# One priority block fewer for every pair but the first, and an earlier fetch of the last four tiles of x

## The chip, the cores and the metric

The kernel runs on one core of a Trainium2 chip. The metric is the device time of one execution in microseconds, median of several runs. PE is TensorE (matrix products), DVE VectorE, ACT ScalarE, POOL GpSimd and SP SyncE, which here only issues DMAs. Each engine works through its own queue in a fixed order and waits there for semaphores.

## What is computed

One layer of an encoder on 1024 tokens of 1024 features, all in float32: a feed-forward at half weight, a mixing layer (bidirectional retention and neighbourhood attention behind one combined projection), and a second feed-forward at half weight, each between two RMS norms. The change concerns the feed-forwards:

```python
def _rms_norm(x, gain):
    xf = x.astype(jnp.float32)
    y = xf * lax.rsqrt(jnp.mean(xf * xf, axis=-1, keepdims=True) + RMS_EPS)
    return (y * gain.astype(jnp.float32)).astype(x.dtype)

def _swiglu(x, w_in, w_out):
    g, u = jnp.split(x @ w_in, 2, axis=-1)
    return (jax.nn.silu(g) * u) @ w_out
...
        h = _swiglu(_rms_norm(x, ffn1_pre_norm[l]), ffn1_w_in[l], ffn1_w_out[l])
        x = x + 0.5 * _rms_norm(h, ffn1_post_norm[l])
...
        h = _swiglu(_rms_norm(x, ffn2_pre_norm[l]), ffn2_w_in[l], ffn2_w_out[l])
        x = x + 0.5 * _rms_norm(h, ffn2_post_norm[l])
```

`w_in` is 1024 x 5632 and `w_out` 2816 x 1024.

## The kernel before

**Products.** A float32 number is split into a high part h, rounded to the format in which PE is fast, and the rest l: a cast on ACT (L61) and a subtraction on DVE (L62), or on POOL where the code says so. A product of two split operands is three matmuls, h·h, h·l and l·h (`mm3`, L86 to L90). Large products use Winograd's form of Strassen's scheme: the operands are cut into quarters, and seven products of combined quarters replace eight. The combined left operands are called a11, a12, a22, s1, s2, s3 and s4.

**The input half of a feed-forward** (`ffn_in`, L517) runs over 22 pairs. Pair i is a block of 128 gate columns and the 128 up columns that belong to it. `Pairs.run` (L476) fetches the pair's two weight blocks g and u (`raw`, three buffers `wraw`, 512 KB each), forms the four combinations t1 (L490), t2 (L491), t3 (L499) and t4 (L508) on DVE, splits each right operand when its product needs it (`piece`, seven buffers `wh` and seven `wl`), and makes the products in the order a11, s2, a12, s3, s1, a22, s4. Each has 12 matmuls of 512 columns into one of six PSUM banks. After each, DVE adds the bank into the result (L494, L497, L502, L505 and L506, L510, L513). `done` applies SiLU to a gate half (ACT, L530) and multiplies it by the up half (DVE, L532) into the tile `gt`, which has three buffers. L473 holds t1 and t3 of a pair on DVE behind the s3 sum (L502) of the pair before.

For some pairs the products a11 and a12 are made ahead by `lead` (L436), before all left operands exist: pairs 0 to 2 are held in PSUM, further ones are saved (7 pairs in all in the first feed-forward, 4 in the second). Those pairs have five products left.

**The factors.** The gated result is the left operand of the output half. Two pairs (a couple) give one block of rows, for which `LeftFactors` makes the seven operands a11 to s4: four sums or differences (DVE, L557) and seven splits (ACT, L577, four buffers `gth`; DVE, L578), each of which POOL's queue stores to DRAM in two DMAs (L68; tensors g0a, g0s in the first feed-forward, g1a, g1s in the second). They are traced one by one between the products of the following pair (`between`, `step`), and what is left when the following pair is finished is traced at once (`drain`).

**The output half** (`ffn_out`) loads quarters of `w_out` (tiles x in the first feed-forward, w in the second), splits them (`wh<-x`, `wl<-x`), loads the stored factors (`g`) and multiplies. Its first three operands are built in a block with offset 80, and the last couple's sums and factors are put behind them on their engines.

**What sets the order.** The queue of each engine is fixed when the program is built. Every instruction gets a number in the order in which the code traces it. The planner goes through a modelled time line; an engine that is free takes, of the instructions that are ready by the model, the one with the lowest number. `high_priority(offset=n)` sets the counter back by n at its start, and at its end restores the value that it had at the start. With offset 0 the instructions inside keep their numbers, but what follows the block starts again from the number of the block's beginning. In `ffn_in` every pair stands in such a block (L533): offset 40 for pair 0, offset 0 for all others. The numbers of neighbouring pairs therefore overlap almost wholly, since only what is traced outside the block moves the counter on. The mixing layer uses the same `Pairs.run` without a block (L1332).

**The beginning** (`first_factors`, L298). SP fetches the first four tiles of x by rows, then in turn four pieces of the transposed x (X^T) for the first 512 tokens (`load(0, k)`, tiles b) and, by `amid`, three weight blocks of W, those of pairs 3, 4 and 5 (`fetch`). For the first two of them `fetch` also makes the first split, on POOL. The norm of the first half comes from sums of squares on ACT and DVE; the scaled X^T is split into a11 and a12. Then the last four tiles of x are fetched as eight halves (tiles `cmb` and `lead`, L355) and squared on ACT (L356), and the second half of X^T is fetched (L359). `rstd(1)` (L360, with L326 on DVE) needs all eight sums. After that s3, s2, s1, a22 and s4 are made.

Of the kernel before, what the change touches and what calls it, by code (L numbers as in the profile page):

```python
# [1 line left out]

# [1 line left out]

# [14 lines left out]
P = 128  # L19
# [217 lines left out]
class Winograd:  # L237
# [25 lines left out]
    def put(self, t, g, pt):  # L263
        c, nc = self.c, self.c.nc
        ts = slice((t % 4) * P, (t % 4 + 1) * P)
        if t < 4:
            c.split(*self.part(("a11", "a12")[g], ts), pt)
            return

        def tmp():  # L270
            return self.tmp.tile([P, 4, P], F32, tag="cmb", name="cmb", bufs=4)

        h1, l1 = [q.bitcast(F32) for q in self.part("a11", ts)]
        h2, l2 = [q.bitcast(F32) for q in self.part("a12", ts)]

        if g == 0:
            self.a21, self.s3 = tmp(), tmp()
            nc.scalar.copy(self.a21, pt)
            if self.spill is not None:
                c.store(self.spill[:, :, ts], self.a21)  # L280
            eng = nc.gpsimd if t in self.s3_on_pool else nc.vector
            eng.tensor_tensor(self.s3, h1, self.a21, ALU.subtract)
            eng.tensor_tensor(self.s3, self.s3, l1, ALU.add)
            return
        a21, s3 = self.a21, self.s3
        s1 = a21 if self.spill is None else tmp()
        c.split(*self.part("a22", ts), pt)
        nc.vector.tensor_tensor(s1, pt, a21, ALU.add)
        c.split(*self.part("s3", ts), s3)
        nc.vector.tensor_tensor(s3, pt, s3, ALU.subtract)  # L290
        c.split(*self.part("s1", ts), s1)
        c.split(*self.part("s2", ts), s3)
        nc.gpsimd.tensor_tensor(s3, h2, s3, ALU.subtract)
        nc.gpsimd.tensor_tensor(s3, s3, l2, ALU.add)
        return lambda: c.split(*self.part("s4", ts), s3, eng=nc.gpsimd)


def first_factors(c, wx, pool, halves, small, x, xt, gain, amid):  # L298

    nc = c.nc
    tt, stt = nc.vector.tensor_tensor, nc.vector.scalar_tensor_tensor
    col, ss = small[:, :KT], small[:, KT:KT + 4 * 4].rearrange("p (q t) -> p q t", q=4)
    blocks = {n: pool.tile([P, 4, 512], F32, name=n) for n in ("b11", "b21", "b22", "b12")}
    rows = [blocks[n].rearrange("p (t k) f -> p t (k f)", t=2)[:, t] for n in ("b21", "b22") for t in range(2)]

    def quarter(h, k):
        return blocks[("b11", "b12", "b21", "b22")[2 * h + k // 4]]

    def block(h, k):
        return quarter(h, k)[:, k % 4]

    def part(n, k):
        return [q[:, k] for q in wx.op(n)]

    def load(h, k):

        nc.sync.dma_start(quarter(h, k)[:, k % 4:k % 4 + 2], xt[h, k // 2])

    def rstd(h):

        rb = c.bank("pt", 2)
        with c.tc.high_priority(offset=100):
            if h:
                tt(ss[:, 1], ss[:, 1], ss[:, 2], ALU.add)  # L326
            nc.vector.tensor_scalar(ss[:, h], ss[:, h], EPS, None, ALU.add)
            r = c.rstd(ss[:, h], 4)
            for t in range(4):
                nc.tensor.transpose(rb[:, t * P:(t + 1) * P], r[:, t:t + 1].to_broadcast([P, P]), c.ident)  # L330
        return rb

    def scale(h, k, rb):
        stt(block(h, k), block(h, k), col[:, k:k + 1], rb, op0=ALU.mult, op1=ALU.mult)

    for t in range(4):
        nc.sync.dma_start(rows[t], x[t * P:(t + 1) * P, :])
    nc.sync.dma_start(col, gain)
    for t in range(4):
        out = ss[:, 0, t:t + 1]  # L340
        if t % 2:
            nc.vector.tensor_tensor_reduce(rows[t], rows[t], rows[t], scale=1.0 / D, scalar=0.0, op0=ALU.mult,
                                           op1=ALU.add, accum_out=out)
        else:
            nc.scalar.activation(rows[t], rows[t], AF.Square, scale=1.0 / 32.0, accum_out=out)
    rb = rstd(0)
    for k in range(0, KT, 2):
        load(0, k)
        amid(k // 2)
    for k in range(KT):  # L350
        scale(0, k, rb)
        c.split(*part(("a11", "a12")[k // 4], k % 4), block(0, k))
    for t in range(4):
        for b in range(2):
            nc.sync.dma_start(halves[t][b], x[(t + 4) * P:(t + 5) * P, b * 512:(b + 1) * 512])  # L355
            nc.scalar.activation(halves[t][b], halves[t][b], AF.Square, scale=1.0 / 32.0,  # L356
                                 accum_out=ss[:, 1 + b, t:t + 1])
    for k in (0, 4, 2, 6):
        load(1, k)  # L359
    rb = rstd(1)  # L360
    yield


    for k in range(4):
        a11, a12, a21, a22 = block(0, k), block(0, k + 4), block(1, k), block(1, k + 4)
        scale(1, k, rb)
        scale(1, k + 4, rb)
        tt(a11, a11, a21, ALU.subtract)
        c.split(*part("s3", k), a11)
        tt(a11, a22, a11, ALU.subtract)  # L370
        c.split(*part("s2", k), a11)
        yield
    for k in range(4):
        a21, a22 = block(1, k), block(1, k + 4)
        tt(a21, a21, a22, ALU.add)
        c.split(*part("s1", k), a21)
    for k in range(4):
        a11, a12, a22 = block(0, k), block(0, k + 4), block(1, k + 4)
        c.split(*part("a22", k), a22)
        nc.gpsimd.tensor_tensor(a12, a12, a11, ALU.subtract)  # L380
        c.split(*part("s4", k), a12, eng=nc.gpsimd)
# [132 lines left out]
        done(2)  # L514


def ffn_in(c, pairs, pool, put):  # L517


    nc = c.nc  # L520
    pairs.between = put.step
    pairs.end, last = None, []
    for i in range(FT):
        gate = [pool.tile([P, 512], F32, tag=f"c{j}", name=f"c{j}", bufs=2) for j in range(2)]
        gt = pool.tile([P, S], F32, tag="gt", name="gt", bufs=3)
        up = gt[:, :512], gt[:, 512:]

        def done(j):
            if j < 2:
                nc.scalar.activation(gate[j], gate[j], AF.Silu)  # L530
            if j in (1, 2):
                last[:] = [pairs.end, nc.vector.tensor_tensor(up[j % 2], gate[j % 2], up[j % 2], ALU.mult).ins]  # L532
        with c.tc.high_priority(offset=0 if i else 40):  # L533
            pairs.run(i, (*gate, *up).__getitem__, done)
        put(i, gt)
    put.drain()
    return last + put.traced
# [634 lines left out]
def trunk_layer(ctx: ExitStack, tc, x, xt, g1a, w1i, w1o, g1b, gma, wmt, wnv, wrv, logits, dtab, rope, bias,  # L1172
                wro, wno, wmo, gmb, g2a, w2i, w2o, g2b, out):
    nc = tc.nc
# [5 lines left out]
    c = Core(tc, const, wpool, psum, dram)  # L1180
# [6 lines left out]
    gl = [{n: dram.tile([FT // 2, P, 1024], F32, name=f"g{i}{n}") for n in Winograd.NAMES} for i in range(2)]  # L1187
# [14 lines left out]
    def pool(stack, name, side="left"):  # L1202
        return stack.enter_context(tc.tile_pool(name=name, bufs=1, side=side, reuse_waits="tile"))
# [3 lines left out]
    early = pool(right, "early", "right")  # L1207
    wx = Winograd(c, apool, early, None, order=("s4", "a22", "s3", "a12", "s1", "s2", "a11"))
    with tc.tile_pool(name="norm1", bufs=1, reuse_waits="tile") as ep:
        def lead():  # L1210
            return early.tile([P, 512], F32, tag="lead", name="lead", bufs=6)

        halves = [[early.tile([P, 4, P], F32, tag="cmb", name="cmb", bufs=4).rearrange("p k t -> p (k t)")
                   for _ in range(2)] for _ in range(2)] + [[lead() for _ in range(2)] for _ in range(2)]
        fin = Pairs(c, wx, [(w1i[i], w1i[FT + i]) for i in LeftFactors.order], 3, 3)
        steps = first_factors(c, wx, ep, halves, pad, x, xt, g1a,
                              lambda j: j < 3 and fin.fetch(3 + j, nc.gpsimd if j < 2 else None))
        next(steps)
        fin.lead(lead, [lambda: next(steps)] * 4, (3, 4, 0), 2, 1)
        for _ in steps:  # L1220
            pass
    g0 = pool(left, "gl10")
    with tc.tile_pool(name="fin1", bufs=1, reuse_waits="tile") as fp:
        tail = ffn_in(c, fin, fp, LeftFactors(c, early, fp, gl[0]))
    right.close()

    spool = pool(left, "s1")
# [10 lines left out]
    ahead = {}  # L1238
# [217 lines left out]
    with tc.tile_pool(name="ep2", bufs=1, reuse_waits="tile") as ep:  # L1456
        rest = c.out_proj(KT, stream(c, gs, lambda k: d["m"][k]), lambda k: c.load_w(wmo[k]),
                          Ep(c, ep, gmb, g2a, False, rows(x1), rows(x2), wx.put))
        fin = Pairs(c, wx, [(w2i[i], w2i[FT + i]) for i in LeftFactors.order], 3, 1)
# [9 lines left out]
    with tc.tile_pool(name="fin2", bufs=1, reuse_waits="tile") as fp:  # L1469
        tail = ffn_in(c, fin, fp, LeftFactors(c, cmb, fp, gl[1]))  # L1470
# [90 lines left out]
```

## Time and profile before

| | |
|---|---|
| median of 3 runs | 2355.51 us (2354.34 to 2355.54) |
| the profiled execution's own time | 2359.59 us |
| its span, first to last instruction | 2357.8 us |
| mean granted PE clock | 0.980 |
| DMA over the span | 444.11 MB, 188 GB/s |

The first feed-forward's input half runs from about 60 to 480 us, its output half to about 700; the mixing layer follows until about 1700; the second feed-forward's input half runs from there to about 2130.

The page gives the busy time of each engine; a profile of one execution is a list of instructions with start and length, and what ended the idle time before each, inferred from semaphores. "[6.06 <-ACT wh L61]" behind a row says that the engine was idle for 6.06 us and that a cast by ACT into `wh`, line 61, ended that. Matmuls overlap, so a full PE shows them 0.222 us apart though each is listed with about 0.39 us. A few matmul records can be missing. A table of stretches gives for each engine the busy time and, behind the x, the number of instructions.

### The profile page before, as it was taken

How to read it: one execution, taken by the hardware profiler on the slowest of the kernel's cores; microseconds unless marked ns; L12 is line 12 of the kernel's file. 1: busy time of each engine (PE TensorE's matmuls, PEld its weight loads, DVE VectorE, ACT ScalarE, POOL GpSimd, SP SyncE). 2: the span in 40 equal slices, each digit the busy share in tenths (PEclk: the TensorE clock that was granted, in tenths of full speed). 3: DMA queues.
4: the chain of work that ended last, by engine and by line, in shares of the span. 5: the costliest groups of instructions: out<-in, count | busy, mean ns of one | idle time of the engine just before them, and what ended most of it. 6: DMA issues, size and time to landing. Idle time of an engine off the chain costs nothing.

```text
span 2357.8 us, 30279 instructions
## 1 busy us (share of the span) xinstructions
PE 2237.6 (95%) x10232; PEld 1838.0 (78%) x10232; DVE 1683.4 (71%) x2918; ACT 1007.2 (43%) x2086; POOL 660.2 (28%) x789
## 2 busy tenths in 40 slices
PE   6989999989998999999999999999898999998997
PEld 4767888868886887777888888887577887887886
DVE  7787977754458668869876677448977897775444
ACT  5333433332335223248876675226533343333232
POOL 3021221158624134411001222002501122115942
PEclk9999999989999999999999999999898999999999
DMA  6253443598645442267654576856434354349864
GB/s 224 97 176 125 173 170 121 190 367 295 205 161 187 170 165 99 102 195 229 217 186 145 164 217 227 312 184 213 129 108 155 130 188 160 131 171 346 303 231 167
DMA packets 149514, 444.11 MB, mean 188 GB/s; under 512 B 18736, under 2 KB 46512, under 8 KB 147248
## 3 DMA queue, kind: packets, MB, share of 16 engines
q1 hardware_dynamic: 110640, 314.23, 39.7%
q0 software_dynamic: 38720, 127.96, 14.3%
q8 instruction: 81, 1.33, 0.2%
q14 instruction: 73, 0.60, 0.1%
HBM read 305.80 MB, written 140.51 MB: 189 GB/s over the span
## 4 chain that ended last, share of the span: by engine, by line
PE 51%; issue 23%; DVE 9%; POOL 6%; DMA 3%; ACT 2%; POOLq 0%; SPq 0%; DVEq 0%; ACTq 0%
PE ps L88 15%; PE ps L90 15%; PE ps L89 15%; DVE wl L62 2%; POOL g1s L68 1%; PE pt L90 1%; PE pt L88 1%; PE pt L89 1%; POOL g1a L68 1%; POOL g0s L68 1%; POOL g0a L68 1%; PE ps L887 1%; PE pt L906 1%; DMA wraw<-in_dram 1%; DMA g<-g0a 1%
## 5 line engine op out<-in xcount | busy, mean ns | idle before, releaser
L62 DVE TENSOR_TENSOR wl<-wraw,wh 128x512 fp32r<-128x512 f32 x510 | 366.9, 742 | 131.7 <-ACT wh L61 129.8
L61 ACT CAST wh<-wraw 128x512 fp32r<-128x512 f32 x516 | 302.8, 618 | 339.9 <-PE ps L89 135.2
L88 PE MATMUL ps<-wh,g 128*128 128x512 f32 x484 | 190.5, 395 | 13.8 <-ACT wh L61 13.8
L89 PE MATMUL ps<-wl,g 128*128 128x512 f32 x484 | 190.7, 394 | 4.6 <-DVE wl L62 4.6
L90 PE MATMUL ps<-wh,g 128*128 128x512 f32 x484 | 190.0, 393 | 0.0
L62 DVE TENSOR_TENSOR wl<-x,wh 128x512 fp32r<-128x512 f32 x77 | 73.8, 974 | 93.2 <-ACT wh L61 93.0
L62 DVE TENSOR_TENSOR wl<-w,wh 128x512 fp32r<-128x512 f32 x77 | 70.5, 929 | 97.5 <-ACT wh L61 97.4
L88 PE MATMUL ps<-a11h,wh 128*128 128x512 f32 x276 | 112.0, 406 | 7.2 <-ACT wh L61 7.2
L88 PEld LDWEIGHTS ps<-wh,g 128*128 128x128 f32 x484 | 92.0, 190 | 33.9 <-ACT wh L61 14.9
L88 PE MATMUL ps<-s2h,wh 128*128 128x512 f32 x232 | 94.5, 407 | 18.9 <-ACT wh L61 15.1
L89 PEld LDWEIGHTS ps<-wl,g 128*128 128x128 f32 x484 | 91.9, 190 | 25.1 <-DVE wl L62 6.1
L90 PE MATMUL ps<-a11h,wl 128*128 128x512 f32 x276 | 110.5, 401 | 0.9 <-POOL wl L62 0.8
L89 PE MATMUL ps<-a11l,wh 128*128 128x512 f32 x276 | 109.9, 399 | 0.0
L90 PE MATMUL ps<-a12h,wl 128*128 128x512 f32 x276 | 108.1, 392 | 1.9 <-DVE wl L62 1.9
L88 PE MATMUL ps<-a22h,wh 128*128 128x512 f32 x280 | 109.7, 392 | 0.0
L88 PE MATMUL ps<-a12h,wh 128*128 128x512 f32 x276 | 108.9, 395 | 0.6 <-DVE gt L506 0.6
L89 PE MATMUL ps<-a22l,wh 128*128 128x512 f32 x280 | 109.1, 390 | 0.0
L90 PE MATMUL ps<-a22h,wl 128*128 128x512 f32 x280 | 109.0, 389 | 0.0
L89 PE MATMUL ps<-a12l,wh 128*128 128x512 f32 x276 | 107.9, 391 | 0.2 <-DVE a12l L62 0.2
L90 PEld LDWEIGHTS ps<-wh,g 128*128 128x128 f32 x484 | 92.0, 190 | 19.1
L61 ACT CAST wh<-t 128x512 fp32r<-128x512 f32 x58 | 36.0, 621 | 149.1 <-DVE t L491 147.9
L61 ACT CAST wh<-w 128x512 fp32r<-128x512 f32 x77 | 46.8, 620 | 117.6 <-PE pt L90 52.8
(424 smaller groups left out, 6497.4 us busy)
## 6 DMA issues: line engine op xcount, KB each, us to landing
wraw<-in_dram SPq DMA_DIRECT2D x218, 512.0 KB, 4.1
g<-g0s SPq DMA_DIRECT2D x44, 512.0 KB, 4.4
g<-g1s SPq DMA_DIRECT2D x44, 512.0 KB, 4.5
g<-g0a SPq DMA_DIRECT2D x33, 512.0 KB, 3.4
g<-g1a SPq DMA_DIRECT2D x33, 512.0 KB, 4.5
g0s<-gth POOLq DMA_DIRECT2D x44, 256.0 KB, 3.0
g0s<-cmb POOLq DMA_DIRECT2D x44, 256.0 KB, 2.8
g1s<-gth POOLq DMA_DIRECT2D x44, 256.0 KB, 3.1
```

The lines of the kernel that those rows point to most:

```text
L61: self.done = [nc.scalar.copy(h, src).ins, (eng or nc.vector).tensor_tensor(l, src, hf, ALU.subtract).ins]
L62: (eng or nc.vector).tensor_tensor(l, src, hf, ALU.subtract).ins]
L68: self.nc.gpsimd.dma_start(dst, src)
L88: mm(ps, a[0], b[0], start=start, stop=False)
L89: mm(ps, a[0], b[1], start=False, stop=False)
L90: mm(ps, a[1], b[0], start=False, stop=stop)
L887: nc.tensor.matmul(bv, q[:, rg * P:(rg + 1) * P], k, start=n == 0, stop=n == 1)
L906: nc.tensor.transpose(pt[:, j * P:(j + 1) * P], s[:, i % 2, (i // 2) * P:(i // 2 + 1) * P], c.ident)
```

## The change

Two things. `ffn_in` gets a parameter `ahead`, by default 0: only pair 0, and only where `ahead` is given, is built in a priority block; all others are traced without one. The first feed-forward passes 40, the second nothing. In `first_factors` the fetches of the last four tiles of x come before the third block of W, and before the scaling of the first half; the second half of X^T is fetched directly behind that block of W. The squares stay where they were.

```diff
-from contextlib import ExitStack
+from contextlib import ExitStack, nullcontext
...
     for k in range(0, KT, 2):
         load(0, k)
-        amid(k // 2)
+        if k < 4:
+            amid(k // 2)
+    for t in range(4):
+        for b in range(2):
+            nc.sync.dma_start(halves[t][b], x[(t + 4) * P:(t + 5) * P, b * 512:(b + 1) * 512])
+    amid(2)
+    for k in (0, 4, 2, 6):
+        load(1, k)
     for k in range(KT):
         scale(0, k, rb)
         c.split(*part(("a11", "a12")[k // 4], k % 4), block(0, k))
     for t in range(4):
         for b in range(2):
-            nc.sync.dma_start(halves[t][b], x[(t + 4) * P:(t + 5) * P, b * 512:(b + 1) * 512])
             nc.scalar.activation(halves[t][b], halves[t][b], AF.Square, scale=1.0 / 32.0,
                                  accum_out=ss[:, 1 + b, t:t + 1])
-    for k in (0, 4, 2, 6):
-        load(1, k)
     rb = rstd(1)
...
-def ffn_in(c, pairs, pool, put):
+def ffn_in(c, pairs, pool, put, ahead=0):
...
-        with c.tc.high_priority(offset=0 if i else 40):
+        with c.tc.high_priority(offset=ahead) if ahead and i == 0 else nullcontext():
             pairs.run(i, (*gate, *up).__getitem__, done)
...
-                              lambda j: j < 3 and fin.fetch(3 + j, nc.gpsimd if j < 2 else None))
+                              lambda j: fin.fetch(3 + j, nc.gpsimd if j < 2 else None))
...
-        tail = ffn_in(c, fin, fp, LeftFactors(c, early, fp, gl[0]))
+        tail = ffn_in(c, fin, fp, LeftFactors(c, early, fp, gl[0]), 40)
```

The second feed-forward's call stays as it is, so its pair 0 loses the block with offset 40.

## The prediction

> **What bounds the kernel now.** I read the page's busy shares first, then the table of stretches, which is where this change can be priced.
>
> ```profile
> span 2357.8 us, 30279 instructions
> PE 2237.6 (95%) x10232; PEld 1838.0 (78%) x10232; DVE 1683.4 (71%) x2918; ACT 1007.2 (43%) x2086; POOL 660.2 (28%) x789
> ```
>
> TensorE is the bound over the whole span: nothing that shortens another engine pays unless it fills a hole on PE. So the next view is PE by stretches. The columns are stretch, length, busy us and count of PE, weight load, DVE, ACT, POOL, then granted clock, DMA share, GB/s.
>
> ```profile
> 80.00:100.00 20.00, 20.00 (x90) 16.58 (x89) 17.95 (x30) 7.56 (x14) 1.30 (x2) 1.00 0.24 81
> 120.00:180.00 60.00, 51.23 (x200) 39.36 (x199) 54.14 (x90) 25.08 (x44) 15.00 (x28) 0.91 0.50 176
> 180.00:460.00 280.00, 276.45 (x1211) 226.17 (x1210) 224.85 (x364) 110.08 (x194) 52.65 (x98) 1.00 0.42 148
> 460.00:500.00 40.00, 28.88 (x115) 22.75 (x114) 27.44 (x44) 15.02 (x27) 13.41 (x25) 0.83 0.87 332
> 1760.00:1800.00 40.00, 31.62 (x116) 24.55 (x116) 36.11 (x60) 19.04 (x35) 14.48 (x27) 0.83 0.60 217
> 1800.00:2120.00 320.00, 317.60 (x1391) 260.09 (x1391) 251.55 (x407) 122.61 (x216) 54.85 (x102) 1.00 0.42 148
> 2120.00:2140.00 20.00, 12.73 (x44) 9.67 (x43) 15.77 (x27) 9.36 (x17) 7.50 (x15) 0.74 0.69 252
> ```
>
> A full stretch has 90 matmuls in 20 us, 0.222 us each. Against that rate the four bad stretches are short of 70 matmuls (270 due in 60 us, 200 there), 65, 64 and 46: **15.6, 14.4, 14.2 and 10.2 us, 54.4 us in all**. Idle time makes up 8.8, 11.1, 8.4 and 7.3 of it, 35.6 us; the rest is the lower granted clock (0.74 to 0.91) in the same stretches. The two long stretches between them lose only 3.6 and 2.4 us of idle time. All four lie inside `ffn_in` or at its end, where the change acts.
>
> Why are there holes? The kernel builds each pair in a block that sets the priority counter back when it ends, so pairs 1, 2, 3 ... carry nearly the same numbers, and the last product of a pair (s4, L512) stands behind the first ones of the next pairs. The stretches for the tile s4h alone show it:
>
> ```profile
> 80.00:95.00 15.00, 2.79 (x8) 1.50 (x8) 0.00 (x0) 0.00 (x0) 1.00 0.26 87
> 95.00:110.00 15.00, 0.78 (x2) 0.38 (x2) 0.00 (x0) 0.00 (x0) 1.00 0.33 123
> 110.00:125.00 15.00, 6.44 (x19) 3.57 (x19) 0.00 (x0) 0.00 (x0) 1.00 0.20 70
> ```
>
> One s4 product shows 8 matmuls of this tile. From 95 to 110 us there are 2, then 19 at once: the s4 of several pairs piled up. DVE starves meanwhile, and then gets everything together:
>
> ```profile
> 122.55 1.29 DVE L513 TENSOR_TENSOR gt<-ps,gt 128x512 f32<-128x512 f32 x2 [12.28 <-PE ps L90]
> ...
> 132.41 0.79 PE L88 MATMUL ps<-s2h,wh 128*128 128x512 f32 x1 [6.06 <-ACT wh L61]
> ...
> 1770.90 0.79 PE L88 MATMUL ps<-s2h,wh 128*128 128x512 f32 x1 [3.67 <-ACT wh L61]
> ...
> 1793.17 0.80 PE L90 MATMUL ps<-s4h,wl 128*128 128x512 f32 x1 [4.71 <-DVE wl L62]
> ```
>
> DVE waits 12.28 us for the late s4, then works off two pairs' sums and factors before it comes to the next pair's weights, and PE waits 6.06 us. The second feed-forward shows the same at 1770.90 and 1793.17. The end of a feed-forward has the other face of it. ACT's rows, then PE's:
>
> ```profile
> 472.67 0.62 ACT L577 CAST gth<-cmb 128x512 fp32r<-128x512 f32 x1 [4.68 <-DMA g0a<-gth]
> 475.36 0.62 ACT L577 CAST gth<-cmb 128x512 fp32r<-128x512 f32 x1 [2.07 <-DMA g0a<-gth]
> 480.73 0.62 ACT L577 CAST gth<-gt 128x512 fp32r<-128x512 f32 x1 [4.75 <-DMA g0s<-gth]
> ...
> 481.78 3.72 ACT L61 CAST wh<-x 128x512 fp32r<-128x512 f32 x7
> ...
> 482.44 0.80 PE L88 MATMUL ps<-wh,g 128*128 128x512 f32 x1 [9.04 <-ACT wh L61]
> ...
> 2130.61 0.79 PE L88 MATMUL ps<-wh,g 128*128 128x512 f32 x1 [4.77 <-ACT wh L61]
> ```
>
> The factors of the last-but-one couple come so late that ACT stands in its queue waiting for their stores to free a `gth` buffer, and the casts that PE needs for `ffn_out` stand behind them.
>
> **The change part by part.** No instruction is added or removed. *Pairs outside the block:* numbers now rise from pair to pair, so s4 of pair i precedes every product of pair i+1 (pair 0 of the first feed-forward keeps its 40). What is then the limit in the pairs whose first two products were made ahead, 7 in the first feed-forward and 4 in the second? PE has 5 products of 12 matmuls, 60 x 0.222 = 13.3 us. DVE has, by the code, 5 weight splits, 4 subtractions, 7 sums, 2 gate products and 5.5 factor operations (11 for two pairs): 23.5. Back to back they come every 0.60 us:
>
> ```profile
> 168.47 1.89 DVE L62 TENSOR_TENSOR wl<-wraw,wh 128x512 fp32r<-128x512 f32 x3
> ```
>
> (1.89 less one length of 0.68, over two.) That is 14.1 us, 0.8 more than PE. So DVE limits these pairs and 7 x 0.8 = 5.6 and 4 x 0.8 = 3.2 us must remain; I leave 6 and 4. Gains: **15.6 - 6 = 9.6 us and 14.2 - 4 = 10.2 us**. Full pairs have 84 matmuls, 18.7 us, and 25.5 operations, 15.3 us: PE limits them and I expect nothing there.
>
> *Ends.* With s4 in place, the last-but-one couple's factors lie in the last two pairs' time, and ACT is free when the first weight blocks land. Bounds for what remains: nothing, as at a change of pair in a plainly ordered stage (next fence), or all of 14.4 and 10.2. I take 3 each, near the first, since the wait in ACT's rows is for these stores alone: **gains 11.4 and 7.2 us**.
>
> How sure is the plain order? The mixing stage runs the same `run` without a block. All of PE, then s4h alone:
>
> ```profile
> 776.00:816.00 40.00, 40.00 (x178) 33.12 (x177) 28.76 (x44) 12.11 (x20) 5.41 (x10) 1.00 0.53 186
> ...
> 776.00:790.00 14.00, 2.69 (x9) 1.50 (x8) 0.00 (x0) 0.00 (x0) 1.00 0.55 194
> 790.00:803.00 13.00, 2.36 (x8) 1.50 (x8) 0.00 (x0) 0.00 (x0) 1.00 0.51 182
> ```
>
> Each pair's s4 is in its place and PE has no hole in 40 us. DVE has less to do there (72% against 80% in 180 to 460), so this is support, not proof.
>
> *Second feed-forward, pair 0 without its 40.* Its first three subtractions now stand behind the factors of the last tokens on DVE:
>
> ```profile
> 1696.25 0.68 DVE L490 TENSOR_TENSOR wraw<-wraw 128x512 f32<-128x512 f32 x1
> ...
> 1701.14 0.68 DVE L491 TENSOR_TENSOR t<-wraw 128x512 f32<-128x512 f32 x1
> ...
> 1703.45 0.68 DVE L499 TENSOR_TENSOR wraw<-wraw 128x512 f32<-128x512 f32 x1
> ...
> 1707.06 0.50 PE L90 MATMUL ps<-s2h,wl 128*128 128x512 f32 x1 [1.54 <-DVE wl L62]
> ```
>
> PE already waits 1.54 us for the split behind them. If the three merely change places with factors that PE also needs, nothing is lost (the factors come 3 x 0.60 = 1.8 us sooner, a gain of that at best); if L490 has to wait until where L499 stands now, the chain moves by 1703.45 - 1696.25 = 7.2 us, the worst case. I take a **loss of 2**, one block of three operations.
>
> *The fetches.* SyncE's queue and what waits for it:
>
> ```profile
> 6.88 0.33 SPq L72 DMA_DIRECT2D wraw<-in_dram  x1
> 8.21 0.33 SPq L319 DMA_DIRECT2D b<-in_dram  x1
> 8.58 3.81 SPq L355 DMA_DIRECT2D cmb<-in_dram  x4
> ...
> 13.35 4.18 SPq L355 DMA_DIRECT2D lead<-in_dram  x4
> 17.94 2.33 SPq L319 DMA_DIRECT2D b<-in_dram  x4
> ...
> 29.76 0.62 ACT L356 ACTIVATE lead<-lead 128x512 f32<-128x512 f32 x1
> ...
> 30.51 0.16 DVE L326 TENSOR_TENSOR edge<-edge 128x4 f32<-128x4 f32 x1 [3.48 <-ACT lead L356]
> ...
> DMA to landing us min/median/max: 5.4/6.3/7.2
> ```
>
> The eight half tiles of x already stand ahead of X^T's second half (17.94). What moves is one block of W, from 6.88 to behind them: x comes earlier by one issue step there, 8.21 - 6.88 = 1.3 us. The last square starts at 29.76, while its tile, issued before 17.94, has landed by 17.94 + 7.2 = 25.1: ACT's order sets it, not the DMA. DVE's wait of 3.48 us can shrink by 1.3 at best. The W block moves past eight tiles in SyncE's queue, some ten us; its casts on ACT and splits on DVE follow it, and PE has the products of the two blocks before until then. If that cover is thinner than I think, I price it at the same 1.3. Between -1.3 and +1.3 I take a **gain of 0.5**, nearer nothing.
>
> Sum: 9.6 + 10.2 + 11.4 + 7.2 - 2 + 0.5 = **36.9 us**. The profiled execution took 2359.59 us (span 2357.8, 1.8 around it) and becomes 2322.7; it is 4.1 above the median of the runs. From the median, 2355.5 - 36.9 = **2318.6 us**.
>
> [...]
>
> **The rivals.** *Slower: the head of every pair waits.* In plain order the next pair's subtractions rank behind this pair's sums and the couple's factors. Where DVE falls behind, PE waits for t2 and its cast at each new pair. Such a wait exists once today:
>
> ```profile
> 202.38 0.50 PE L88 MATMUL ps<-s2h,wh 128*128 128x512 f32 x1 [1.49 <-ACT wh L61]
> ```
>
> At 1.49 us over the 15 + 18 full pairs it costs 49 us: 2355.5 - 36.9 + 49 = 2368. It decides from 36.9 / 33 = 1.1 us per pair. For it: the factors come in bursts. Against it: 276.45 busy of 280 now, DVE with a fifth of its time free, and the mixing stage's 40.00 of 40.
>
> *Half of it:* the holes close in one kind of place alone, because ACT still waits for stores at the ends or DVE's backlog moves on: about 18 us, 2338, anywhere from 2320 to 2350.
>
> *It does not do what it says:* the planner orders by what is ready, and s4 stays late for want of a weight buffer rather than of rank; the four stretches keep their losses: 2355, within 5. Against it: the plain stage's s4.
>
> **How the numbers follow.** Forecast 0.60 (own range 2303 to 2336: 52 us if hardly more than DVE's excess stays lost, 20 us if the ends keep half), half of it 0.17, no effect 0.08, slower 0.15. Below 2300 everything in the four stretches would have to go, 54.4 + 1.3 us; I leave 0.05 there. Above 2362 lies most of the slower case, 0.13. So the range is 2300 to 2362. What a measurement can tell from no change is about 0.2%, 5 us: faster 0.77, same 0.08, slower 0.15.
>
> **What would show it.** Right: s4h with about 8 matmuls in every stretch of one pair, DVE without the 12 us wait near 110, PE back to 90 matmuls in 20 us in the four stretches, ACT casting weights for `ffn_out` before PE ends the last s4. Wrong: new waits of PE for `wh` or `wl` at each s2, or the same gap at the two ends with ACT behind `gth`.

## The result, and the profile after

The changed kernel takes 2303.31 us (median of 4 runs, 2301.5 to 2306.33) against 2355.53 for the kernel before (median of 4 runs): the ratio is 0.9779, with a 95% interval of 0.9762 to 0.9796. That is 52.2 us less, where 36.9 were forecast. The profiled execution took 2301.5 us. Its page begins so:

```profile
span 2299.7 us, 30245 instructions
...
PE 2215.9 (96%) x10232; PEld 1831.9 (80%) x10232; DVE 1689.7 (73%) x2918; ACT 1002.6 (44%) x2086; POOL 663.2 (29%) x789
```

The counts of the five engines are those of before: only the order changed. The span is 58.1 us shorter. Here is the table of stretches of the changed kernel, with the columns of the prediction's (stretch, length, then busy us and count of PE, weight load, DVE, ACT and POOL, granted clock, DMA share, GB/s). 2060 to 2080 is added, since the second input half now ends there.

```profile
120.00:180.00 60.00, 55.88 (x239) 45.55 (x238) 56.33 (x93) 26.83 (x47) 15.03 (x28) 0.97 0.54 193
180.00:460.00 280.00, 280.00 (x1237) 231.91 (x1236) 227.62 (x369) 109.49 (x196) 52.69 (x98) 1.00 0.46 165
460.00:500.00 40.00, 40.00 (x178) 33.15 (x177) 26.33 (x30) 15.51 (x27) 25.03 (x24) 1.00 1.02 403
1760.00:1800.00 40.00, 40.00 (x178) 33.16 (x177) 33.59 (x55) 15.83 (x29) 7.80 (x15) 1.00 0.50 182
1800.00:2120.00 320.00, 320.00 (x1413) 264.95 (x1412) 252.43 (x395) 125.56 (x222) 79.58 (x124) 1.00 0.51 188
2120.00:2140.00 20.00, 20.00 (x90) 16.55 (x89) 7.92 (x8) 6.60 (x11) 16.67 (x13) 1.00 0.76 281
2060.00:2080.00 20.00, 20.00 (x89) 16.37 (x89) 10.17 (x17) 5.44 (x11) 1.08 (x2) 1.00 0.71 277
```

PE is full everywhere but in the first stretch. The long ones also give the true rate of a full PE: 280 us for 1237 matmuls and 320 for 1413 are 0.2264 us each. The operands of these matmuls are rounded to fp32r; that PE would be slower with another format, no run here shows. The prediction took 0.222 from a stretch of 20 us, where one or two matmuls that straddle an edge already weigh. In the timeline of the end of the input half, one product takes 2.72 us, which is 0.2267 a matmul; the rows of ACT come first, then those of PE.

```profile
457.69 3.73 ACT L61 CAST wh<-x 128x512 fp32r<-128x512 f32 x7
...
456.23 0.39 PE L88 MATMUL ps<-s4h,wh 128*128 128x512 f32 x1
...
458.72 0.39 PE L90 MATMUL ps<-s4h,wl 128*128 128x512 f32 x1
458.95 0.39 PE L88 MATMUL ps<-wh,g 128*128 128x512 f32 x1
```

ACT casts the weights of the output half from 457.69, before the last s4 matmul at 458.72, and PE goes on without a gap. Before, ACT came to the same casts at 481.78, behind three waits for stores, and PE had stood 9.04 us. s4 alone, in the prediction's three stretches:

```profile
80.00:95.00 15.00, 2.79 (x8) 1.60 (x9) 0.00 (x0) 0.00 (x0) 1.00 0.26 87
95.00:110.00 15.00, 3.77 (x12) 2.29 (x13) 0.00 (x0) 0.00 (x0) 1.00 0.71 253
110.00:125.00 15.00, 2.79 (x10) 1.55 (x9) 0.00 (x0) 0.00 (x0) 1.00 0.54 185
```

The pile of 2 and then 19 has become 8, 12 and 10. DVE, which stood 12.28 us at 122, now works almost throughout; its stretch (DVE's busy us and count, clock, DMA share, GB/s):

```profile
100.00:144.00 44.00, 42.52 (x70) 1.00 0.65 234
```

With 0.2267 us a matmul, the rows of both kernels give what each stretch is short of:

| stretch | short before, us | short after, us | gained | forecast |
|---|---|---|---|---|
| 120 to 180 | 14.7 | 5.8 | 8.9 | 9.6 |
| 180 to 460 | 5.5 | 0 | 5.5 | 0 |
| 460 to 500 (end) | 13.9 | 0 | 13.9 | 11.4 |
| 1760 to 1800 | 13.7 | 0 | 13.7 | 10.2 |
| 1800 to 2120 | 4.7 | 0 | 4.7 | 0 |
| 2120 to 2140 (end) | 10.0 | 0 | 10.0 | 7.2 |

(For example 60 / 0.2267 = 264.7 matmuls due and 239 there: 25.7 x 0.2267 = 5.8.) The sum is 56.7 of the 58.1 us of span. The stretches are fixed in time, and from the second one on the change is ahead, so it does other work in them than the kernel before. Matched matmul by matmul, the two traces give nearly the same gains: 8.9, 5.9, 14.3, 13.9, 4.9 and 10.2. The earlier start is not among them: the first s2 starts 1.2 us earlier (68.18 for 69.36), but by 120 us the change is 0.8 us behind.

What is still lost before 180 us is mostly one hole. The timeline of the changed kernel there, all engines:

```profile
139.77 0.69 DVE L582 TENSOR_TENSOR cmb<-cmb,gth 128x512 fp32r<-128x512 f32 x1
...
140.97 0.69 DVE L494 TENSOR_TENSOR wraw<-wraw 128x512 f32<-128x512 f32 x1
...
142.17 0.69 DVE L495 TENSOR_TENSOR t<-wraw 128x512 f32<-128x512 f32 x1
...
142.95 0.62 ACT L61 CAST wh<-t 128x512 fp32r<-128x512 f32 x1
...
143.62 0.50 PE L88 MATMUL ps<-s2h,wh 128*128 128x512 f32 x1 [3.58 <-ACT wh L61]
```

DVE works without a pause, but the next pair's first subtractions (L494, L495) come behind the couple's factors (L582), and the cast that PE waits for hangs on L495. It is the head-of-pair wait of the prediction's slower rival, in one place.

### The profile page after: what moved, and what is told of

Read it like the earlier page. It is cut to its first block, busy times and chain, and to the rows that moved or that the text cites. A ratio compares the mean times of both kernels' runs of the same rounds, so it can differ in the third digit from the quotient of the medians.

```text
span 2299.7 us, 30245 instructions
## 1 busy us (share of the span) xinstructions
PE 2215.9 (96%) x10232; PEld 1831.9 (80%) x10232; DVE 1689.7 (73%) x2918; ACT 1002.6 (44%) x2086; POOL 663.2 (29%) x789
## 4 chain that ended last, share of the span: by engine, by line
PE 78%; DVE 9%; issue 4%; POOL 2%; DMA 2%; ACT 1%; POOLq 0%; DVEq 0%; SPq 0%; ACTq 0%
PE ps L90 24%; PE ps L88 24%; PE ps L89 24%; DVE wl L62 2%; PE pt L88 1%; PE pt L89 1%; PE pt L90 1%; PE ps L891 1%; PE pt L910 1%; POOL rstd L98 1%; DMA wraw<-in_dram 0%; POOL cmb L294 0%; POOL cmb L293 0%; DVE t L495 0%; DMA kraw<-nk 0%
## 5 line engine op out<-in xcount | busy, mean ns | idle before, releaser
L534 ACT ACTIVATE c<-c 128x512 f32<-128x512 f32 x88 | 55.6, 632 | 218.3 <-DVE c L501 116.3
```

## The experiments

Theory: pairs with overlapping numbers let PE take the next pairs' products ahead of the last one of a pair. Its result and the couple's factors then come late and in a heap, first DVE and then PE stand, and at the end ACT stands behind the factors' stores. Rivals: the fetches do a part of it; s4's own place is enough; DVE's load is the limit. Each ratio is to the kernel before, timed on the same chip.

**The two parts alone.** The first kernel is before with the block edit alone:

```diff
-        with c.tc.high_priority(offset=0 if i else 40):
+        with c.tc.high_priority(offset=ahead) if ahead and i == 0 else nullcontext():
```

> The kernel before with the change of the priority blocks alone; the fetches stand as before. Theory (s4 of each pair back in its place is what pays): nearly the whole gain, 2304 to 2306 us, that is 50 to 52 us under the kernel before. Rival (the earlier fetch of x carries a share, since DVE's wait at 30 us shrinks from 3.48 to 2.25 us in the kernel after): 2307 us or more.

Measured: 2303.11 us, 0.9761 (0.9747 to 0.9775). The second kernel is the change with the old line of blocks put back:

```diff
-        with c.tc.high_priority(offset=ahead) if ahead and i == 0 else nullcontext():
+        with c.tc.high_priority(offset=0 if i else 40):
```

> The kernel before with the change of the fetches alone; all pairs stay in their blocks. Theory: 1 to 2 us faster than before at best, since the first s2 product moves from 69.36 to 68.18 us in the kernel after. Rival (the new start of the first pairs shifts what piles up later): anything from 5 us slower to 8 us faster.

Measured: 2358.57 us, 1.0000 (0.9991 to 1.0008). The fetches do reach the start. The timeline's row of the last sum over the squares, with the fetches alone, against 30.51 in before:

```profile
28.34 0.16 DVE L326 TENSOR_TENSOR edge<-edge 128x4 f32<-128x4 f32 x1 [2.25 <-ACT lead L362]
```

It comes 2.2 us earlier and the first s2 1.1 us (68.23), but the timed median doesn't show it. The whole gain is that of the blocks.

**s4 alone brought forward.** Before, with s4 set back by 100 numbers, first the product alone and then the product and its sum:

```diff
-        p3 = self.product("s4", b22)
+        with c.tc.high_priority(offset=100) if self.lift else nullcontext():
+            p3, = self.products("s4", [b22])
+        self.between()
         self.end = tt(c12, p3, c12, ALU.add).ins
```

> The kernel before, with the pairs in their blocks, but the s4 product of each feed-forward pair set back by 100 numbers, so that it ranks before the next pair's products; its sum and gate product keep their late numbers. Theory that PE's late s4 is the cause: 30 us or more of the 52 come back (below 2325 us). Rival (the overlap of the numbers hurts by the order on DVE and ACT, whatever PE does): less than 15 us come back (above 2340 us).

> As the run before, and the sum after s4, the gate product and what follows it are set back with it. If the late s4 is the cause by way of the late sums and factors: 40 us or more come back (below 2315 us). If the product alone counts: the same time as the run before within 5 us. If DVE's and ACT's order of everything else counts: above 2335 us.

Measured: 2368.79 us, 1.0044 (1.0030 to 1.0058), and 2377.02 us, 1.0074 (1.0061 to 1.0087). By what was expected, the late s4 should have given back 30 or 40 us; both are a little slower than before instead, by 0.4 and 0.7%, which alone would speak for the rival, the order on DVE and ACT. In the first of them the table of stretches for s4h alone has s4 in its place:

```profile
95.00:110.00 15.00, 3.67 (x12) 1.95 (x11) 0.00 (x0) 0.00 (x0) 1.00 0.45 158
110.00:125.00 15.00, 2.62 (x8) 1.50 (x8) 0.00 (x0) 0.00 (x0) 1.00 0.24 87
```

and the same table for a22h, the product before it, has the old pile:

```profile
95.00:110.00 15.00, 0.39 (x1) 0.19 (x1) 0.00 (x0) 0.00 (x0) 1.00 0.45 158
110.00:125.00 15.00, 6.62 (x20) 3.94 (x21) 0.00 (x0) 0.00 (x0) 1.00 0.24 87
```

1 and then 20: a22 has taken s4's part. At the end of the input half ACT's SiLU now waits for DVE's sum of a22 (L511 in that kernel; a row of its timeline):

```profile
475.77 0.63 ACT L534 ACTIVATE c<-c 128x512 f32<-128x512 f32 x1 [10.93 <-DVE c L511]
```

The output half starts at 485.71. So the reading that s4 as such is the late one falls: with s4 ranked first, a22 is the last of its pair, and is pushed behind the next pairs in its place.

**PE in order, numbers as before.** Before, with all its blocks, but each product held on PE behind the last s4 matmul of the pair before (an order on PE alone, no wait for data):

```diff
+                if k == 0 and self.tail is not None:
+                    self.c.tc.add_manual_dep(f.ins, self.tail.name, mybir.DependencyInfo(
+                        mybir.DependencyClass.NoSync, mybir.DependencyReason.DATA), reason="order")
...
         done(2)
+        if self.ordered:
+            self.tail = self.mm.ins
```

> The kernel before with all its blocks, and one thing more: on PE each product of a feed-forward pair is held behind the last s4 matmul of the pair before. The numbers on DVE, ACT and POOL overlap as before. Theory (PE taking the next pair's products ahead of a pair's tail is the cause): 2303 to 2320 us. Rival (the overlapping numbers hurt by the order on DVE and ACT): above 2335 us.

Measured: 2296.66 us, 0.9727 (0.9708 to 0.9746), faster than the 2303 to 2320 expected. Its stretches (PE alone, then clock, DMA share, GB/s):

```profile
80.00:180.00 100.00, 100.00 (x443) 1.00 0.53 182
180.00:440.00 260.00, 260.00 (x1149) 1.00 0.47 160
...
1680.00:2060.00 380.00, 380.00 (x1675) 1.00 0.46 158
```

The first two in the changed kernel:

```profile
80.00:180.00 100.00, 95.23 (x410) 0.98 0.52 184
180.00:440.00 260.00, 260.00 (x1149) 1.00 0.43 154
```

The numbers still overlap, DVE has the same instructions, and yet PE is full in both input halves, without the hole at 143 us. So the order on PE is enough, and overlapping numbers on DVE and ACT don't hurt by themselves. (The edit adds an order on PE alone; the planner then lays out the other queues anew behind it, so they are not those of the kernel before either.) The run also shows that DVE's surplus need not reach PE: where the numbers overlap, DVE may take the next pair's subtractions ahead of the factors.

**Where the gain is made.** The changed kernel with offset-0 blocks for the early pairs only (1 to 5 in the first feed-forward, 0 to 3 in the second), then for the last three pairs only:

```diff
-        with c.tc.high_priority(offset=ahead) if ahead and i == 0 else nullcontext():
+        with (c.tc.high_priority(offset=ahead) if ahead and i == 0 else
+              c.tc.high_priority(offset=0) if i < pairs.held + pairs.saved else nullcontext()):
...
+              c.tc.high_priority(offset=0) if i >= FT - 3 else nullcontext()):
```

> The kernel after, with the old block of offset 0 put back for the pairs whose first products are made ahead alone (pairs 1 to 5 in the first feed-forward, 0 to 3 in the second). Theory: the holes near 130 us and near 1770 us come back, 7 and 13 us, and the ends stay closed: 2315 to 2330 us, PE without idle time at the ends. Rival (it is the sum over all 22 pairs that piles up): within 5 us of the kernel after.

> The kernel after, with the old block of offset 0 put back for the last three pairs of each feed-forward alone. Theory: the gaps at the two ends come back, 14 and 10 us as counted in the kernel before, and all else stays: 2320 to 2330 us, with ACT behind its gth buffers before the first cast for ffn_out. Rival (the ends were late because all pairs were): within 5 us of the kernel after.

Measured: 2328.28 us, 0.9868 (0.9852 to 0.9884), and 2331.63 us, 0.9878 (0.9858 to 0.9897). Blocks for the early pairs bring back the first hole (stretches of that kernel):

```profile
120.00:180.00 60.00, 51.31 (x199) 39.41 (x198) 54.38 (x90) 25.75 (x45) 17.70 (x33) 0.89 0.53 185
180.00:460.00 280.00, 274.39 (x1200) 226.65 (x1199) 232.30 (x377) 112.72 (x200) 57.09 (x106) 0.99 0.43 154
460.00:500.00 40.00, 40.00 (x178) 32.96 (x177) 26.57 (x36) 13.00 (x23) 15.11 (x19) 1.00 1.01 388
```

(199 matmuls from 120 to 180 us where before had 200), and lose something behind it, while the end stays closed. Blocks for the last three pairs bring back the end, with its waits of ACT for stores in the timeline:

```profile
467.72 0.62 ACT L582 CAST gth<-gt 128x512 fp32r<-128x512 f32 x1 [5.52 <-DMA g0s<-gth]
...
468.78 3.72 ACT L61 CAST wh<-x 128x512 fp32r<-128x512 f32 x7
```

while the full pairs ahead of them stay full (stretches of the same kernel):

```profile
180.00:400.00 220.00, 220.00 (x972) 182.25 (x971) 182.88 (x297) 88.63 (x158) 44.71 (x83) 1.00 0.44 157
...
440.00:480.00 40.00, 29.69 (x121) 23.54 (x120) 24.04 (x39) 13.92 (x26) 10.21 (x19) 0.87 0.77 289
```

Against the change the two spans, each of one profiled execution, lose 27.9 us (2327.6 - 2299.7) and 23.5 us (2323.2 - 2299.7), 51.4 of the 58.1: the early pairs and the ends are two separate gains of about one size. That the stores' buffers alone, with more of them, would have closed the ends wasn't tried.

**The one block that stays, and the one that goes.** The changed kernel with 40 for pair 0 of the second feed-forward too, and with no block at all:

```diff
-        tail = ffn_in(c, fin, fp, LeftFactors(c, cmb, fp, gl[1]))
+        tail = ffn_in(c, fin, fp, LeftFactors(c, cmb, fp, gl[1]), 40)
...
-        tail = ffn_in(c, fin, fp, LeftFactors(c, early, fp, gl[0]), 40)
+        tail = ffn_in(c, fin, fp, LeftFactors(c, early, fp, gl[0]))
```

> The kernel after, with offset 40 for pair 0 of the second feed-forward as well, as it was before. Prediction's step (its loss costs 2 us): 2 us faster than the kernel after. What the two traces show (the first s2 came 1 to 2 us sooner without it): 1 to 2 us slower. Rival (it is worth much more): over 5 us either way.

> The changed kernel with the last block (pair 0 of the first feed-forward, set forward by 40) taken away too, so that nothing in either feed-forward is built in a block. Theory A, the whole gain comes from pairs 1 and later having rising numbers, and pair 0's block only decides what its three subtractions and first casts stand behind at the start: the gain stays to within 4 us (2299 to 2308), the first s2 starts between 67 and 72 us, and the first matmul of the first output half stays within 4 us of 458.95. Rival B, the block ahead is needed to cover the start, because pair 0's subtractions fall behind the squares and sums of the last tiles of x: the first s2 comes as much as 7 us later (75 us) and the whole kernel with it, 2310.

Measured: 2306.47 us, 0.9773 (0.9758 to 0.9788), and 2304.86 us, 0.9774 (0.9761 to 0.9788). Neither differs from the change. With 40 the second feed-forward's first s2 starts earlier, and stands again (PE's timeline of that kernel):

```profile
1674.30 0.39 PE L88 MATMUL ps<-s2h,wh 128*128 128x512 f32 x1
...
1676.96 0.50 PE L90 MATMUL ps<-s2h,wl 128*128 128x512 f32 x1 [1.54 <-DVE wl L62]
```

A further stop, of 1.17 us, follows at 1721.66. Without it s2 starts at 1679.46 and runs through; the output half begins at 2077.74 without and at 2078.75 with it. Without any block the first s2 is at 68.28 (68.18 in the change) and the first output half starts at 460.48 (458.95).

**Is DVE's load what is left?** Two edits of the changed kernel. One takes twelve operations off DVE: the four sums and differences of each of the first three couples are replaced by copies of one operand on ACT, so these factors aren't the Winograd combinations. The other leaves the work and gives the products made ahead to pairs 4, 6, 8 and 10 instead of 3 to 6, so that full pairs (seven products) stand between these short ones (five); pairs 0 to 2 stay short, one behind the other.

```diff
+            if j < self.light:
+                return lambda: self.traced.append(c.nc.scalar.copy(a[0], a[1]).ins)
             return lambda: self.traced.append(c.nc.vector.tensor_tensor(*a).ins)
...
-                self.begun[i] = pair
+                self.begun[self.pos.get(i, i)] = pair
...
+        fin.pos = {3: 4, 4: 6, 5: 8, 6: 10}
```

> The kernel after, with the four sums and differences of the factors of the first three couples of the first feed-forward replaced by copies on ACT, so those factors are not the right ones; DVE has 12 operations of 0.60 us less in the first seven pairs, ACT 12 more. If DVE's load is what makes PE wait 3.58 us at 143.62 us in the kernel after: that hole goes and the first feed-forward's output half starts 4 to 7 us sooner than at 458.95 us. If the wait is for a weight block or a buffer: it stays, within 1.5 us of 458.95.

> The kernel after, with the products made ahead of time given to pairs 4, 6, 8 and 10 in place of 3, 4, 5 and 6, so that full pairs (18.7 us of PE, 15.3 of DVE) stand between them. If DVE falls behind because seven short pairs (13.3 of PE, 14.1 of DVE) follow one another: no hole near 143 us, output half sooner than 458.95 by 4 to 7 us. If each short pair costs PE by itself: the same loss, in several small holes.

Measured: 2299.47 us, 0.9753 (0.9740 to 0.9767), and 2295.30 us, 0.9737 (0.9724 to 0.9751). With the lighter factors a hole stays. Rows of that kernel's timeline, ACT, then DVE, then PE:

```profile
137.79 0.62 ACT L584 CAST gth<-cmb 128x512 fp32r<-128x512 f32 x1 [4.25 <-DMA g0a<-gth]
...
138.45 0.69 DVE L585 TENSOR_TENSOR cmb<-cmb,gth 128x512 fp32r<-128x512 f32 x1 [2.79 <-ACT gth L584]
...
139.06 0.68 DVE L494 TENSOR_TENSOR wraw<-wraw 128x512 f32<-128x512 f32 x1
...
141.70 0.50 PE L88 MATMUL ps<-s2h,wh 128*128 128x512 f32 x1 [2.53 <-ACT wh L61]
```

DVE is idle for 2.79 us in front of a factor whose cast ACT hasn't made, with the next pair's subtraction queued behind it. ACT isn't busy in that time: it stands 4.25 us for the store that frees a `gth` buffer. So this edit puts a wait for a buffer in place of DVE's backlog, and doesn't tell how much DVE's amount matters by itself; it shows that a hole remains although DVE has idle time, because of what is queued ahead. The output half starts at 457.31, 1.6 us sooner and not the 4 to 7 expected if DVE's load were the cause. Spread out, the short pairs leave no hole in these stretches (PE's stretches of that kernel):

```profile
80.00:180.00 100.00, 100.00 (x443) 1.00 0.51 182
180.00:440.00 260.00, 260.00 (x1149) 1.00 0.45 160
```

The output half starts at 450.82 instead of 458.95, 8.1 us earlier, a little more than the 4 to 7 expected.

**Both together.** The changed kernel with the order on PE of above, and offset-0 blocks again for every pair but pair 0 of the first feed-forward (40):

```diff
-        with c.tc.high_priority(offset=ahead) if ahead and i == 0 else nullcontext():
+        with c.tc.high_priority(offset=0 if i else ahead):
```

> The kernel after, with PE held in pair order by the link of the run with PE in order, and the old overlap of the numbers put back on the other engines (offset 0 for all pairs but pair 0 of the first feed-forward, which keeps 40; pair 0 of the second has none). Theory (PE needs the order of the pairs, DVE is better off with the next pair's weights ahead of the last pair's factors): no hole in the first pairs of either feed-forward, 2287 to 2294 us, faster than both kernels. Rival (the overlap on DVE only moves its backlog on): 2297 to 2306 us, no better than the kernel after.

Measured: 2293.88 us, 0.9729 (0.9716 to 0.9742), span 2288.1. Its interval lies wholly below the change's (0.9762 to 0.9796). DVE's timeline shows why (L588 is a factor's split, L497 and L498 the next pair's first subtractions):

```profile
130.90 0.68 DVE L497 TENSOR_TENSOR wraw<-wraw 128x512 f32<-128x512 f32 x1
131.50 1.29 DVE L588 TENSOR_TENSOR cmb<-cmb,gth 128x512 fp32r<-128x512 f32 x2
132.70 0.68 DVE L498 TENSOR_TENSOR t<-wraw 128x512 f32<-128x512 f32 x1
...
133.90 0.69 DVE L588 TENSOR_TENSOR gt<-gt,gth 128x512 fp32r<-128x512 f32 x1
```

Factors and subtractions are interleaved, not one behind the other. From the first s2 at 68.11 to the output half at 450.68 it takes 382.6 us; the 1680 matmuls of that half (22 x 84 less 7 x 24) need 380.9 at 0.2267. The change takes 390.8, before 413.1 (69.36 to 482.44). But PE in order alone (69.65 to 452.20) and the spread short pairs (68.15 to 450.82) take 382.6 and 382.7 as well, and their intervals overlap with this kernel's: these runs don't tell which of the three is fastest.

## Why the prediction was right, and where it was off

The direction and its reason held; the sum was 15.3 us too small, and the time lies at the fast end of the forecast's own range (2303 to 2336). That end was to be reached with 52 us from the four bad stretches alone; they gave 46.5 us, and 10.2 came from stretches priced at nothing. That the time still lies inside is in part luck.

- **"s4 of several pairs piled up."** Right as a picture, too narrow as a cause: with s4 brought forward a22 piled up in its place, and the time rose. The cause is that the pairs' numbers overlap and PE follows them; holding PE in order with the numbers unchanged is worth as much as the change, and somewhat more.
- **"90 matmuls in 20 us, 0.222 us each."** The full rate is 0.2267. This overstates the four bad stretches by little (54.4 against 14.7 + 13.9 + 13.7 + 10.0 = 52.3).
- **"Full pairs: I expect nothing there."** The largest miss. At 0.2267 the two long stretches of before, 1211 and 1391 matmuls, are short of 24.3 and 20.8, which is 5.5 + 4.7 = 10.2 us. The rows were quoted, but only their idle time was read (3.6 and 2.4), and none of it was credited. All of it was gained.
- **"DVE limits these pairs and 5.6 and 3.2 us must remain."** The first number was met (5.8 of the 6 left), though by luck: it is one hole, from the order on DVE, and not 0.8 us in each pair. The second was not: in the change the second feed-forward's short pairs run from 1679.46 to about 1735 us with one stop, of 0.53 us, and 13.7 was gained instead of 10.2. With the same DVE work and PE in order, nothing remains in either. There the surplus of 0.8 us a pair was put off; in the change it cost PE where factors were queued ahead of the next pair's weights. The lighter factors, which brought a wait for a buffer, don't settle how much the amount adds.
- **Ends, "I take 3 each".** Nothing remained: 2.5 and 2.8 us more than forecast. The mechanism was as described, and comes back when the last three pairs alone get their blocks.
- **Pair 0 of the second feed-forward, "a loss of 2".** Not there: with the 40 put back the time is the same within the intervals, and the output half starts 1.0 us later, not earlier. The subtractions did come later, as forecast, but the early start ended in stops of 1.54 and 1.17 us.
- **The fetches, "a gain of 0.5".** Right in what can be measured: nothing alone. The last sum came 2.25 us earlier (28.26 for 30.51), more than the 1.3 given as the bound, and the first s2 1.2 us; by 120 us that lead was gone. "ACT's order sets it, not the DMA" was right, but the change moved ACT's order too: before, two casts of weights (at 20.90 and 21.95 us) stood ahead of squares and ACT waited 1.36 us for DVE at 24.54; in the change these casts come behind the last square, from 29.55 on, and that wait is gone.
- **The slower rival.** A wait at the head of every pair does not exist: PE is busy 280.00 of 280 us from 180 to 460. It does exist in the short pairs in a row, as the hole at 143.62, after a stretch in which DVE was busy 42.52 of 44 us. The half-size rival's times are those of the two kernels with blocks for the early or the last pairs, 2328 and 2332; the change has both halves. And the change does what it says: s4 is in its place.
- **"The rest is the lower granted clock."** The four bad stretches were short of 52.3 us by the counts, 35.6 of them idle time; the other 16.7 are missing in stretches whose granted clocks were 0.91, 0.83, 0.83 and 0.74. The sum was made from counts, so they were in it; from idle time alone they would have been left out. In the change the granted clock is 0.97 in the first of the four and 1.00 in the other three.

The median gained 52.2 us and the profiled span 58.1: the profiled execution of before was 4.1 us above the median of its runs, that of the change was 1.8 below (2301.5 against 2303.31).

## What to carry to other kernels

A priority block that restores its counter gives the next iteration the same numbers, so whatever ranks last in an iteration is pushed behind the next ones: look at one tile's count per stretch, for every product and not only the one that catches the eye. When such an overlap is removed, check what it had been good for; here it also put the next weights ahead of work that could wait, and the two kernels that fix the order on PE alone and leave the overlap to the other engines are faster than the change. Spreading the short pairs did as well. Price a stretch by a count against a rate from a long full stretch, and read the long, nearly full ones as well: the 600 us that looked full held 10.2 of the 58.1 gained.

## What was not expected of the hardware

Behind a short stop of PE its clock was lower for longer than the stop had lasted. In before, PE stood 1.77 us, and its timeline then reads:

```profile
150.98 0.50 PE L88 MATMUL ps<-s2h,wh 128*128 128x512 f32 x1 [1.77 <-ACT wh L61]
...
152.69 0.63 PE L90 MATMUL ps<-s2h,wl 128*128 128x512 f32 x1
153.12 0.63 PE L88 MATMUL ps<-s2h,wh 128*128 128x512 f32 x1
...
156.27 0.39 PE L90 MATMUL ps<-s3h,wl 128*128 128x512 f32 x1
156.50 0.39 PE L88 MATMUL ps<-s3h,wh 128*128 128x512 f32 x1
```

From 152.69 the matmuls come 0.43 us apart, and 0.23 apart again from about 155.6. The granted clock says the same (PE's stretches of before):

```profile
151.00:156.00 5.00, 5.00 (x14) 0.66 0.28 105
```

In the kernel with the block edit alone, the first s2 follows a longer stop, of 2.69 us, at 69.57, and costs no clock (PE's stretches of that kernel):

```profile
69.50:75.50 6.00, 5.93 (x26) 1.00 0.16 27
```

A stop of 2.18 us, at 1446.71 in the change, costs none either: the matmuls of 512 columns behind it come 0.23 us apart, and the granted clock is 1.00 from 1446.7 to 1452.7. So between about 1.8 and 2.7 us the length of the stop doesn't decide alone; what else does, no run shows. The hole of 3.58 us in the change is dearer for it: the s4 product ahead of it begins at 137.16 and the product behind s2 at 148.86, 11.7 us for two products that need 5.4, so 6.3 us are lost, of which 3.58 and 0.55 are idle; the other 2.1 are the slower spacing behind (0.43 us from 145.49 to 148.05; the granted clock is 0.76 from 143 to 150).
